# A re-searched written order up to LayerNorm 1, and the first blocks of x and context issued behind SiLU

## The chip, the cores and the metric

The kernel runs on one core of a Trainium2 chip. A core has a matrix engine (TensorE, PE in the profile), a vector engine (VectorE, DVE), a scalar engine (ScalarE, ACT), GpSimd (POOL) and SyncE (SP), each with an instruction queue of its own that runs in order. Sixteen DMA engines move data between memory and the on-chip buffer; here SP issues nearly all transfers, ScalarE a few. The metric is the device time of one execution in microseconds, the median of three runs.

## The reference

One layer of a diffusion backbone, in float32, over 256 latent tokens `x` and 256 context tokens `ctx`, width 2048. The layer computes

- `m = silu(cond) @ w_ada + b_ada`, for the sample's conditioning vector `c` and for the context's `c_ctx`, split into six vectors (shift, scale and gate for the mixer, and the same for the feed-forward part);
- `h = (x * (1 + scale) + shift) @ w_in` for latent and context tokens, the combined q/k/v projection: 3072 columns, two groups of 8 query heads with 2 key and 2 value heads each;
- attention: group A within a window with a sink logit, group B global with RMS-normalised q and k, both with axial rotary positions, keys being the latent keys and all context keys;
- `x = LayerNorm(alpha * x + gate1 * (heads @ w_out))`, LayerNorm 1;
- `x = LayerNorm(alpha * x + gate2 * ((silu(u @ w_gate) * (u @ w_up)) @ w_down))` with `u = x * (1 + scale2) + shift2`, hidden width 5632, LayerNorm 2.

## The kernel before, in words

Every large product is done as three matmuls of a float32 value split into a high and a low part: `hi*hi`, `lo*hi`, `hi*lo` (lines 240 to 242). The high part of a weight tile is a cast on ScalarE (`hi<-raw`, line 507 up to LayerNorm 1, line 230 after it), the low part a subtraction on VectorE (`lo<-raw,hi`, lines 510 and 231). The modulated tokens are split in the same way (`uh`, `ul`, lines 741 and 744).

Up to LayerNorm 1 the work is a list of about 1250 steps, each added with `F.add` for one engine. `Flow.run` goes through the string `PLAN` and emits the steps in that order; each engine keeps it (the region is a manual schedule), and steps of different engines wait for each other through semaphores only. A number is a step; a letter behind it says which pool a load takes its buffer from (`r`: four buffers, `a`: two). `wN` emits N warm-up matmuls of 128 columns into a spare bank (line 1253); each shows as two instructions in the trace.

The q/k/v projection runs over groups of the 16 blocks of 128 input columns: 2, 2, 4 and 8 blocks. For each group the shift and scale columns are computed from `w_ada` (line 558), then x and context are turned by TensorE (line 728), modulated (734), split, and multiplied with `w_in`. Ahead of the list stand the loads of the conditioning rows, a transposition of them (line 291), SiLU on ScalarE (line 294) and a tile of ones (line 306).

The steps around the start that the prediction speaks of:

| Step | Engine | What it does |
|---|---|---|
| 2, 4, 6, 8 | SP | the four first loads of w_ada, 1 MB each |
| 3, 5, 7, 9 | PE | their products with the conditioning columns, 16 matmuls each (line 558); 3 and 5 need loads 2 and 4, 7 needs 6, 9 needs 8 |
| 10 | ACT | copy of the sums (line 589), after 9 |
| 11 | PE | the sums turned into columns (line 594), after 10 |
| 0, 1 | PE, ACT | the bias b_ada transposed (line 454) and copied (line 457) |
| 12, 13 | DVE | shift and scale, from 11 and 1 (lines 600, 602) |
| 14; 19 | PE | flip of the first x block; of the first context block (line 728) |
| 15, 16, 17, 18 | ACT, ACT, ACT, DVE | x: two modulations, `uh`, `ul` |
| 20, 21, 22, 23 | ACT, ACT, ACT, DVE | the same for the context |
| 60, 67, 49, 85, 92, 78 | SP | loads of w_in for block rows 0 and 1; their casts are 61, 68, 50, 86, 93, 79 |
| 63, 70 | PE | products with the weights of 60 and of 67, the first of the old and of the new order |
| 37, 38 | ACT queue | loads of x and of the context for block group 2 (lines 699, 704) |
| 946, 1195 | POOL | two memsets |
| 1192, 1193 | SP, PE | loads of the LayerNorm rows, and their transposition |

A part of how a modulation step waits, which the table cannot say:

```python
p = F.add("PE", 205 * nj, flip, (), [ps], at=-1.0, since=9500.0)
for j in range(nj):
    p = F.add("ACT", 460, lambda j=j, f=modulate: f(j), [p] + ready, [uf] if j == 0 else [], [ps])
```

The numbers given to `F.add` were the planner's costs and due times when the order was searched for; in the kernel only the list `PLAN` decides.

After LayerNorm 1 come the gate, up and down projections in a fixed order of their own, which is the same in both kernels.

Of the kernel before, what the change touches and what calls it, by code (L numbers as in the profile page):

```python
# [21 lines left out]
P = 128  # L22
# [43 lines left out]


PLAN = """
4r 2r 1195 6a w6 3 5 0 w3 7 19 8a 946 w7 9 60r 10 1 61 14 11 1192 67r 49r 155a 27a 85r 13 12 15 16 17 20 50 68 21 22
62 18 51 w12 63 64 69 52 56 86 38 23 65 66 87 70 55 74 72 76 37 89 59 28r 78r 79 80 31r 30r 116 137r 1193 73 77 29 71  # L70
88 1194 91 156 157 32 53 33 138 99a 148r 100r 39 34 75 36 35 139 81 83 40 41 82 54 90 58 44 101 45 46 42 102r 103a 149
47 43 158 141 150 105r 92r 106a 93 162 151 104 48 57 84 145 142 143 140 144 147 94 166r 108r 109a 167 107 152 160 153
168 146 164 169 170 154 171 180r 181 182 172 110 96 115 225a 111 184 122 132 127 173r 112 95 98 226 227 228 113 114
174 175 294r 187a 188r 229 186 133 97 123 161 297 165 298 159 117 177 179 176 163 124 183 189 118 134 119 120 295 296
178 121 300 304 128 129 125 301 126 230r 231 185 315r 130 308 299 303 232 307 135 136 318 302 131 233 319 316 306 305
309 310 235a 190r 191a 311 313 312 321 234 317 236 238 237 239 192 328r 329 320 323 325 322 330 240r 314 331 242 332
334 324 338 333 337 342 349r 327 335 339 350 352 326 241 244 353 351 243 193r 245a 194r 246 247 248 250a 362r 255r 249
251 252 254 341 345 346 354 343 355 195 336 347 340 344 365 366 348 363 364 368 357 359 356 358 367 370 369 260r 196r
197r 375a 203 371 372 360 373 361 198 199 204 388 200 210 205 272 24 947 273 257 253 256 259 258 262 261 264 263 202
# [32 lines left out]
1235 1236 1161 1162 1163 1242 1164 1233 1183 1221 1222 1184 1185 1165 1189 1190 1223 1224a 1230r 1243 1225 1244 1226a  # L112
1228r 1234 1191 1227 1229 1231
"""


# [47 lines left out]
def dit_layer(ctx: ExitStack, tc: tile.TileContext, x, c, cx, c_ctx, w_ada, b_ada, w_in, q_norm_g,  # L164
              k_norm_g, sink_logit, w_out, ln1_g, ln1_b, w_gate, w_up, w_down, ln2_g, ln2_b,
              rope_cos, rope_sin, out):
    nc = tc.nc
    x, c, cx = x[0], c, cx[0]
# [11 lines left out]
    def wk_bank():  # L180
        return wk_ps.tile([P, NB], F32, tag="wk", name="wk")
# [17 lines left out]
    xt = main.tile([P, NT, D], F32, tag="xt", name="xt")  # L199
# [82 lines left out]
    brow = pa.tile([6 * KD, P], F32, tag="brow", name="brow")  # L282
    nc.scalar.dma_start(brow, b_ada.rearrange("o (n p) -> (o n) p", p=P))
    first_cx = xt[:, :, D - 2 * P :]
    nc.scalar.dma_start(xt[:, :, : 2 * P], x[:, : 2 * P].rearrange("(t p) d -> p t d", p=P))
    nc.scalar.dma_start(first_cx, cx[:, : 2 * P].rearrange("(t p) d -> p t d", p=P))
    early = wk_bank()
    for _ in range(EARLY_WARM):
        nc.tensor.matmul(early[:, :P], lhsT=ident, rhs=ident, start=True, stop=True)
# [14 lines left out]
    nc.vector.reduce_sum(fold, ident.rearrange("p (a i) -> p i a", a=4), axis=AX.X)  # L304
    ones_r = main.tile([P, P], F32R, tag="ones", name="ones")
    nc.scalar.activation(ones_r, ident, AF.Copy, bias=1.0, scale=0.0)
    ones = ones_r.bitcast(F32)


# [1556 lines left out]
```

## Time and profile before

| What | Value |
|---|---|
| median of three runs | 1119.51 us (1116.37 to 1120.67) |
| profiled execution | 1117.67 us, span 1115.9 us |
| TensorE busy | 1095.1 us, 98% of the span |
| VectorE, ScalarE busy | 895.3 us (80%), 602.6 us (54%) |
| DMA | 321.24 MB, mean 288 GB/s |
| first product of the q/k/v projection | 22.72 us after the span's start |
| last matmul | 1103.06 us after the span's start |

The span goes from the first to the last instruction; the execution's time is some microseconds longer. In the timeline a row has its start, its duration, the engine, the line, the operation, what it writes and reads, and a count; in brackets stands the idle time before it and what ended that. ACTq and SPq are the issues of transfers on the queues of ScalarE and SP. Matmuls overlap, so the time from one start to the next says more than the duration. Line numbers are those of the kernel before.

### The profile page before, as it was taken

How to read it: one execution, taken by the hardware profiler on the slowest of the kernel's cores; microseconds unless marked ns; L12 is line 12 of the kernel's file. 1: busy time of each engine (PE TensorE's matmuls, PEld its weight loads, DVE VectorE, ACT ScalarE, POOL GpSimd, SP SyncE). 2: the span in 40 equal slices, each digit the busy share in tenths (PEclk: the TensorE clock that was granted, in tenths of full speed). 3: DMA queues.
4: the chain of work that ended last, by engine and by line, in shares of the span. 5: the costliest groups of instructions: out<-in, count | busy, mean ns of one | idle time of the engine just before them, and what ended most of it. 6: DMA issues, size and time to landing. Idle time of an engine off the chain costs nothing.

```text
span 1115.9 us, 13859 instructions
## 1 busy us (share of the span) xinstructions
PE 1095.1 (98%) x5121; PEld 886.5 (79%) x5121; DVE 895.3 (80%) x1075; ACT 602.6 (54%) x874; POOL 39.4 (4%) x86
## 2 busy tenths in 40 slices
PE   7999999999999999999999999999999999999995
PEld 6677788778878788888888888888888788888884
DVE  2469999999998898877667776887875899578886
ACT  3345675786765356445465455555644565445541
POOL 1000040102000010000000000000000000000000
PEclk9999999999999999999999999999999999999998
DMA  9999998889999789989768798899896575536651
GB/s 336 383 401 392 392 338 323 298 270 315 330 323 365 275 311 357 336 295 345 265 209 280 272 342 280 295 317 312 302 308 224 174 251 206 198 141 236 233 209 75
DMA packets 175273, 321.24 MB, mean 288 GB/s; under 512 B 8899, under 2 KB 46691, under 8 KB 172901
## 3 DMA queue, kind: packets, MB, share of 16 engines
q1 hardware_dynamic: 173718, 319.23, 81.5%
q10 hardware_dynamic: 1264, 1.11, 0.3%
q8 instruction: 40, 0.66, 0.2%
q14 instruction: 27, 0.22, 0.1%
q0 software_dynamic: 224, 0.02, 0.0%
HBM read 304.07 MB, written 16.25 MB: 287 GB/s over the span
## 4 chain that ended last, share of the span: by engine, by line
PE 93%; DVE 4%; DMA 2%; ACT 1%; issue 0%; SPq 0%; DVEq 0%; ACTq 0%
PE acc L240 22%; PE acc L242 22%; PE acc L241 22%; PE wk L242 7%; PE wk L241 7%; PE wk L240 7%; PE wk L1036 2%; PE wk L558 2%; DMA raw<-in_w_ada_dram 2%; DVE adav L359 1%; PE wk L728 1%; DMA adav<-in_b_ada_dram 1%; PE acc L1253 0%; DVE lo L237 0%; DVE m L986 0%
## 5 line engine op out<-in xcount | busy, mean ns | idle before, releaser
L231 DVE TENSOR_TENSOR lo<-raw,hi 128x1024 fp32r<-128x1024 f32 x232 | 281.1, 1222 | 126.7 <-ACT hi L230 124.8
L230 ACT CAST hi<-raw 128x1024 fp32r<-128x1024 f32 x232 | 243.8, 1055 | 242.3 <-PE acc L242 130.2
L240 PE MATMUL acc<-hi,u2h 128*128 128x512 f32 x448 | 175.4, 391 | 0.0
L242 PE MATMUL acc<-hi,u2l 128*128 128x512 f32 x448 | 174.8, 390 | 0.3 <-DVE u2l L1579 0.3
L241 PE MATMUL acc<-lo,u2h 128*128 128x512 f32 x448 | 174.7, 390 | 0.0
L359 DVE SCALAR_TENSOR_TENSOR adav<-raw,cs,adav 128x1024 f32<-128x1024 f32 (+1 forms) x96 | 114.4, 1191 | 6.3 <-DMA raw<-in_w_ada_dram 2.9
L507 ACT CAST hi<-raw 128x1024 fp32r<-128x1024 f32 x84 | 87.7, 1052 | 57.8 <-PE acc L242 36.8
L510 DVE TENSOR_TENSOR lo<-raw,hi 128x1024 fp32r<-128x1024 f32 x84 | 101.3, 1222 | 10.5 <-ACT hi L507 10.3
L240 PE MATMUL acc<-hi,hTh 128*128 128x512 f32 x264 | 102.8, 390 | 0.6 <-ACT hi L236 0.6
L240 PE MATMUL acc<-hi,uh 128*128 128x512 f32 x256 | 102.9, 402 | 0.0
L241 PE MATMUL acc<-lo,hTh 128*128 128x512 f32 x264 | 102.8, 390 | 0.0
L242 PE MATMUL acc<-hi,hTl 128*128 128x512 f32 x264 | 102.7, 390 | 0.0
L242 PE MATMUL acc<-hi,ul 128*128 128x512 f32 x256 | 100.3, 392 | 0.0
L241 PE MATMUL acc<-lo,uh 128*128 128x512 f32 x256 | 99.9, 390 | 0.0
L242 PE MATMUL wk<-hi,u2l 128*128 128x512 f32 x256 | 99.8, 390 | 0.0
L241 PE MATMUL wk<-lo,u2h 128*128 128x512 f32 x256 | 99.8, 390 | 0.0
L240 PE MATMUL wk<-hi,u2h 128*128 128x512 f32 x256 | 99.7, 390 | 0.0
L242 PEld LDWEIGHTS acc<-hi,u2l 128*128 128x128 f32 x448 | 84.2, 188 | 18.1 <-DVE u2l L1579 0.7
L240 PEld LDWEIGHTS acc<-hi,u2h 128*128 128x128 f32 x448 | 84.2, 188 | 18.1 <-ACT u2h L1578 0.8
L241 PEld LDWEIGHTS acc<-lo,u2h 128*128 128x128 f32 x448 | 84.2, 188 | 17.6 <-DVE lo L231 0.4
L240 PEld LDWEIGHTS acc<-hi,uh 128*128 128x128 f32 x256 | 48.2, 188 | 15.6 <-issue 2.1
L240 PEld LDWEIGHTS acc<-hi,hTh 128*128 128x128 f32 x264 | 49.6, 188 | 11.3 <-ACT hi L236 1.0
(296 smaller groups left out, 1730.3 us busy)
## 6 DMA issues: line engine op xcount, KB each, us to landing
raw<-in_w_ada_dram SPq DMA_DIRECT2D x64, 1024.0 KB, 8.1
raw<-in_w_gate_dram SPq DMA_DIRECT2D x44, 1024.0 KB, 6.5
raw<-in_w_up_dram SPq DMA_DIRECT2D x44, 1024.0 KB, 5.5
raw<-in_w_down_dram SPq DMA_DIRECT2D x44, 1024.0 KB, 5.2
raw<-in_w_ada_dram SPq DMA_DIRECT2D x64, 512.0 KB, 5.9
raw<-in_w_in_dram SPq DMA_DIRECT2D x18, 1024.0 KB, 7.9
raw<-in_w_out_dram SPq DMA_DIRECT2D x16, 1024.0 KB, 7.1
pd<-hx SPq DMA_DIRECT2D x64, 128.0 KB, 5.3
```

The lines of the kernel that those rows point to most:

```text
L230: nc.scalar.copy(hi[:, :n], raw[:, s : s + n])
L231: nc.vector.tensor_tensor(lo[:, :n], raw[:, s : s + n], hi[:, :n].bitcast(F32), op=ALU.subtract)
L240: nc.tensor.matmul(ps, lhsT=xh, rhs=w[0], start=first, stop=False, skip_group_check=seeded)
L241: nc.tensor.matmul(ps, lhsT=xh, rhs=w[1], start=False, stop=False, skip_group_check=seeded)
L242: nc.tensor.matmul(ps, lhsT=xl, rhs=w[0], start=False, stop=last, skip_group_check=seeded)
L359: nc.vector.scalar_tensor_tensor(a[:, c : c + piece], raw[:, f : f + piece], cs[:, 4 * (g * (G4 * NB // w) + j) + 2, None], a[:, c : c + p ...
L507: nc.scalar.copy(hl.hi[:, :n], raw.t[:, s : s + n])
L510: nc.vector.tensor_tensor(hl.lo[:, :n], raw.t[:, s : s + n], hl.hi[:, :n].bitcast(F32), op=ALU.subtract)
L558: nc.tensor.matmul(bank.t[32 * j : 32 * j + 32, :width], lhsT=cs[:, 4 * k + 2 - 2 * i : 4 * k + 34 - 2 * i], rhs=raw.t[:, c * width : (c + ...
L728: nc.tensor.transpose(ps.t[:, (j * 2 + t) * P : (j * 2 + t + 1) * P], src, ident)
L1036: nc.tensor.matmul(o_ps.t[:, : 2 * P].rearrange("p (g q) -> p g q", q=32), lhsT=v, rhs=pv[:, k], start=k == 0, stop=k == 3)
```

## The change

Two edits. First, the two transfers of the first blocks of x and of the context, which ScalarE's queue issued ahead of the table load, SiLU and the ones tile, are issued behind these. Second, the string `PLAN` is replaced by another order of the same steps, with 29 units of warm-up instead of 28. No computation is added or removed. The string is cut here to its first lines.

```diff
 PLAN = """
-4r 2r 1195 6a w6 3 5 0 w3 7 19 8a 946 w7 9 60r 10 1 61 14 11 1192 67r 49r 155a 27a 85r 13 12 15 16 17 20 50 68 21 22
-62 18 51 w12 63 64 69 52 56 86 38 23 65 66 87 70 55 74 72 76 37 89 59 28r 78r 79 80 31r 30r 116 137r 1193 73 77 29 71
...
+4a 2a w11 3 6r 1195 8r 14 5 w5 7 w11 9 10 37 67r 68 946 49r 1192 85r w2 11 0 19 1 38 13 12 50 51 69 28a 27a 92r 15 16
+86 17 18 87 20 21 70 88 22 23 54 74 89 1193 72 90 76 93 52 94 58 1194 91 29 53 95 56 96 78r 30r 79 80 31r 155a 166r
...
 """
```

```diff
     brow = pa.tile([6 * KD, P], F32, tag="brow", name="brow")
     nc.scalar.dma_start(brow, b_ada.rearrange("o (n p) -> (o n) p", p=P))
     first_cx = xt[:, :, D - 2 * P :]
-    nc.scalar.dma_start(xt[:, :, : 2 * P], x[:, : 2 * P].rearrange("(t p) d -> p t d", p=P))
-    nc.scalar.dma_start(first_cx, cx[:, : 2 * P].rearrange("(t p) d -> p t d", p=P))
...
     ones_r = main.tile([P, P], F32R, tag="ones", name="ones")
     nc.scalar.activation(ones_r, ident, AF.Copy, bias=1.0, scale=0.0)
+    nc.scalar.dma_start(xt[:, :, : 2 * P], x[:, : 2 * P].rearrange("(t p) d -> p t d", p=P))
+    nc.scalar.dma_start(first_cx, cx[:, : 2 * P].rearrange("(t p) d -> p t d", p=P))
     ones = ones_r.bitcast(F32)
```

More of the change, by code (lines that the diff above doesn't have):

```diff
@@ L68 @@
 PLAN = """
-4r 2r 1195 6a w6 3 5 0 w3 7 19 8a 946 w7 9 60r 10 1 61 14 11 1192 67r 49r 155a 27a 85r 13 12 15 16 17 20 50 68 21 22
-62 18 51 w12 63 64 69 52 56 86 38 23 65 66 87 70 55 74 72 76 37 89 59 28r 78r 79 80 31r 30r 116 137r 1193 73 77 29 71
-88 1194 91 156 157 32 53 33 138 99a 148r 100r 39 34 75 36 35 139 81 83 40 41 82 54 90 58 44 101 45 46 42 102r 103a 149
-47 43 158 141 150 105r 92r 106a 93 162 151 104 48 57 84 145 142 143 140 144 147 94 166r 108r 109a 167 107 152 160 153
-168 146 164 169 170 154 171 180r 181 182 172 110 96 115 225a 111 184 122 132 127 173r 112 95 98 226 227 228 113 114
@@ L74 @@
[L74 to L78, printed above, removed]
@@ L79 @@
-197r 375a 203 371 372 360 373 361 198 199 204 388 200 210 205 272 24 947 273 257 253 256 259 258 262 261 264 263 202
[32 rows of a table removed]
-1235 1236 1161 1162 1163 1242 1164 1233 1183 1221 1222 1184 1185 1165 1189 1190 1223 1224a 1230r 1243 1225 1244 1226a
-1228r 1234 1191 1227 1229 1231
+4a 2a w11 3 6r 1195 8r 14 5 w5 7 w11 9 10 37 67r 68 946 49r 1192 85r w2 11 0 19 1 38 13 12 50 51 69 28a 27a 92r 15 16
+86 17 18 87 20 21 70 88 22 23 54 74 89 1193 72 90 76 93 52 94 58 1194 91 29 53 95 56 96 78r 30r 79 80 31r 155a 166r
@@ new lines @@
+100a 60r 97 156 157 98 57 32 81 33 82 44 39 34 35 36 61 83 84 62 71 55 59 99r 101 102r 103a 148r 63 75 45 167 40 41 46
+47 42 48 160 43 164 168 65 64 73 66 104 158 137a 105r 115 180r 138 181 139 140 144 77 141 162 182 169 170 171 172 149
+161 183 225a 108r 106a 109r 226 145 150 184 152 227 185 229 154 107 142 228 186 146 143 165 147 110 151 153 294r 295
+111 297 116 298 173a 117 112 122 315r 187r 230r 188a 174 113 114 175 296 159 132 177 179 176 127 300 123 124 118 119
+120 121 304 316 163 317 125 299 320 322 126 308 303 189 318 231 319 235a 240r 328r 232 233 236 234 178 312 190r 191a
@@ new lines @@
+321 128 129 130 133 134 135 136 131 324 307 301 237 238 311 323 329 325 305 302 326 306 309 239 330 333 331 332 337
+192 310 349r 327 334 313 352 350 341 336 345 314 338 340 342 344 335 355 348 354 245a 194r 193r 242 241 244 243 246
+247 248 353 351 195 356 339 357 343 359 358 250a 362r 255r 249 251 252 254 365 366 363 346 347 367 368 364 369 370 371
+373 361 372 260r 196r 197r 374 360 198 199 200 375a 203 204 210 205 215 257 253 256 259 258 262 261 263 264 201 202
[32 rows of a table added]
+1238 1221 1161 1236 1163 1162 1234 1222 1242 1239 1182 1183 1184 1185 1189 1164 1190 1165 1230r 1228a 1224a 1226r 1243
@@ L114 @@
+1191 1223 1244 1225 1227 1229 1231
 """
```

64 rows, old and new, of the table PLAN are left out of this document.

## The prediction

> **What bounds the kernel now.** I read the page first, then TensorE's waits, then the timeline of the first 24 us, then stretches of the span.
>
> ```profile
> PE 1095.1 (98%) x5121; PEld 886.5 (79%) x5121; DVE 895.3 (80%) x1075; ACT 602.6 (54%) x874; POOL 39.4 (4%) x86
> ```
>
> The waits of TensorE (total us, times, longest) after the first weights are there:
>
> ```profile
> PE wk L558 <- DMA raw<-in_w_ada_dram: 1.2, 1, 1.2
> PE wk L594 <- ACT ada L589: 0.7, 1, 0.7
> ...
> PE wk L1036 <- ACT pr L998: 0.3, 1, 0.3
> ```
>
> TensorE is the bound, and it hardly ever waits: 0.7 and 0.3 us between its first product and LayerNorm 1. The sum of its work is the same under the new order. So the question is when the first product of the q/k/v projection starts, and whether TensorE stalls later. TensorE's timeline up to that product (start, us, line):
>
> ```profile
> 7.76 0.28 PE L291 MATMUL wk<-ident,crow 32*128 32x32 f32 x1 [3.04 <-DMA crow<-in_c_ctx_dram]
> 7.97 2.93 PE L1253 MATMUL acc<-ident 128*128 128x128 f32 x12
> 12.07 1.93 PE L558 MATMUL wk<-raw,cs 128*32 128x256 f32 x32 [1.17 <-DMA raw<-in_w_ada_dram]
> 13.94 0.30 PE L454 MATMUL wk<-ident,brow 96*128 96x96 f32 x1
> ...
> 14.86 1.07 PE L558 MATMUL wk<-raw,cs 128*32 128x256 f32 x16
> 15.87 0.66 PE L728 MATMUL wk<-ident,xt 128*128 128x128 f32 x4
> 16.36 1.73 PE L1253 MATMUL acc<-ident 128*128 128x128 f32 x14
> 18.01 1.07 PE L558 MATMUL wk<-raw,cs 128*32 128x256 f32 x16
> 19.02 0.66 PE L728 MATMUL wk<-ident,xt 128*128 128x128 f32 x4
> 19.57 0.61 PE L594 MATMUL wk<-sel,ada 128*128 128x4 f32 x4
> 20.04 2.92 PE L1253 MATMUL acc<-ident 128*128 128x128 f32 x24
> 22.72 0.47 PE L240 MATMUL acc<-hi,uh 128*128 128x512 f32 x1
> ...
> 23.26 0.40 PE L242 MATMUL acc<-hi,ul 128*128 128x512 f32 x1
> ```
>
> L1253 are warm-up matmuls, two per unit of a "w" word; L558 with 256 columns are the four steps 3, 5 (together at 12.07), 7 and 9, that multiply the first w_ada loads; L728 are the flips of the first blocks of context and x. Before, step 9 ends at 19.02 and the first product starts at 22.72. ScalarE and VectorE in between:
>
> ```profile
> 2.46 0.58 ACTq L285 DMA_DIRECT2D xt<-in_x_dram  x1
> ...
> 3.07 1.00 ACTq L286 DMA_DIRECT2D xt<-in_ctx_dram  x1
> ...
> 8.17 0.30 ACT L306 ACTIVATE ones<-ident 128x128 fp32r<-128x128 f32 x1
> ...
> 19.15 0.37 ACT L589 COPY ada<-wk 128x256 f32<-128x256 f32 x1 [10.68 <-PE wk L558]
> ...
> 19.42 0.25 ACT L457 COPY bcol<-wk 128x96 f32<-128x96 f32 x1
> 19.55 1.06 ACT L507 CAST hi<-raw 128x1024 fp32r<-128x1024 f32 x1
> ...
> 21.68 0.62 ACT L741 CAST uh<-uf 128x512 fp32r<-128x512 f32 x1
> ...
> 22.33 0.69 DVE L744 TENSOR_TENSOR ul<-uf,uh 128x512 fp32r<-128x512 f32 x1 [0.47 <-ACT uh L741]
> 22.67 1.99 ACT L507 CAST hi<-raw 128x1024 fp32r<-128x1024 f32 x2
> ```
>
> From the copy of the modulation sums (19.15) to the finished uh (21.68 + 0.62 = 22.30) ScalarE needs 3.15 us; the first product follows its copy by 3.57, as the 24 warm-ups stand ahead of it on TensorE.
>
> **The change, part by part.**
>
> *The two transfers on ScalarE's queue.* They go behind SiLU and the ones tile (8.17), so x is issued at about 8.3 instead of 2.46 and the context at about 8.9. Leaving the front of that queue they free nothing on the path: SiLU waits for the transposition at 7.76, which waits for the row of c_ctx. When x lands comes from the issues up to 40 us (line, KB each, us from issue to landing):
>
> ```profile
> raw<-in_w_in_dram SPq DMA_DIRECT2D x8, 512.0 KB, 7.0
> xt<-in_x_dram ACTq DMA_DIRECT2D x2, 256.0 KB, 7.2
> ...
> xt<-in_ctx_dram ACTq DMA_DIRECT2D x1, 256.0 KB, 8.7
> cxt<-in_ctx_dram ACTq DMA_DIRECT2D x1, 256.0 KB, 6.2
> ...
> crow<-in_c_ctx_dram ACTq DMA_DIRECT2D x1, 8.0 KB, 6.4
> ```
>
> Whoever stood alone on the queue took 6.2 or 6.4; the first blocks took longer behind three others. I take 6.4: x lands at 14.7. The bounds are 13.3 (no wait at all, see below) and 8.3 + 8.7 = 17.0.
>
> [...]
>
> *TensorE's new order up to step 9* is w11, 3, flip of x, 5, w5, 7, w11, 9. The first 12 warm-ups take 2.93 us at 7.97 and 24 take 2.92 at 20.04, so early ones run at half the rate: w11 (22 of them) lasts until 12.6 if all of it is slow and about 12 if the rate rises on the way. I start step 3 at 12.3, its loads having landed by 12.07 even before. One group of 16 lasts 1.01 (14.86 to 15.87), a flip 0.49 (15.87 to 16.36), 14 warm-ups 1.65 (16.36 to 18.01), 0.118 each.
> - Step 3: 12.3 to 13.3. Then TensorE waits for x until 14.7; queued behind are step 5, both warm-up words, 7 and 9, and ScalarE's copy behind 9.
> - Flip of x to 15.2; step 5 to 16.2; w5 to 17.4; step 7 to 18.4; w11 to 21.0; step 9 to 22.0.
>
> That is 22.0 against 19.02: **+3.0**. Even with x there at 13.3, step 9 ends at 20.6, since 32 warm-ups and a flip now stand between the groups. That the w_ada loads may land earlier, with 0.5 MB less beside them, is worth nothing: TensorE comes to the last two at 17.4 and 21.0.
>
> *From step 9 to the first product.* ScalarE's new order is copy, issue of x block 2, cast, bias copy, issue of context block 2, cast, two modulations, cast, uh. Before, there is one cast ahead of uh, now three: two more of 1.0 each (22.67: 1.99 for two). The issues moved here cost the queue this much each:
>
> ```profile
> 27.10 0.59 ACT L793 COPY kvacc<-acc 128x512 f32<-128x512 f32 x1 [1.33 <-PE acc L242]
> 27.22 0.38 ACTq L704 DMA_DIRECT2D cxt<-in_ctx_dram  x1
> ...
> 27.58 1.05 ACT L507 CAST hi<-raw 128x1024 fp32r<-128x1024 f32 x1
> ```
>
> With an issue between, the cast starts 0.48 after the copy ahead of it; without one 0.13 to 0.27. Two issues: +0.5, part of it hidden under the copies. So 3.15 + 2.0 + 0.5 = 5.65 from copy to uh, against the 3.57 after which the first product used to start: **+2.1**. The bias transposition, now behind the sums, is ready 1.3 after the copy (sums 19.57 to 20.04, then a 0.30 transposition, as at 13.94) and the cast ahead of the bias copy ends at 1.5, so it hides; gone that cover, it would cost some tenths. The third cast's weights are issued when step 7 frees its buffer (18.4) and land 7.0 us later, 1 us ahead of their cast. I count nothing.
>
> *ul.* It is ready 0.72 after uh's end (22.33 + 0.69 less 22.30); the third matmul wants it 0.54 after the first: **+0.2**.
>
> *The rest of the order to LayerNorm 1.* There is 1.0 us of TensorE's waits to win back (0.7 and 0.3). To lose: runs of products are broken 59 times instead of 53, while all changes from one kind of TensorE work to another are 146 instead of 145. A break costs about 0.1 (14 warm-ups at the 0.112 of those from 20.04 to 22.72 end at 17.93, the group behind them starts at 18.01); I allow 0.2. Bounds −1.0 and +1.2; I take 0, as the two counts pull against each other. The block loads moved ahead have no reader before 40 us.
>
> **Sum:** 3.0 + 2.1 + 0.2 = 5.3 us. The profiled execution took 1117.67 us (span 1115.9), so it would be 1122.97; it lies 1.84 below the median of the runs, 1119.51, and on that footing the forecast is **1124.8 us**. With the bounds of x (−1.4, +2.3) and of the rest, 1122.4 to 1128.3.
>
> **The rivals.**
>
> *The clock falls back.* TensorE's last work ahead of the first product, the context's flip, ends about 2.0 after the copy; the product starts at 5.65, after 3.6 us with no warm-up in them. What idleness does stands at the span's end (last matmul; then TensorE's busy time first, granted clock third from the right):
>
> ```profile
> 1103.06 0.39 PE L242 MATMUL acc<-hilo,hTl 128*128 128x512 f32 x1
> ```
> ```profile
> 1103.00:1106.00 3.00, 0.45 (x2) 0.03 (x1) 2.38 (x5) 0.00 (x0) 0.00 (x0) 1.00 0.05 18
> 1106.00:1107.00 1.00, 0.00 (x0) 0.00 (x0) 0.89 (x7) 0.00 (x0) 0.00 (x0) 0.90 0.00 0
> ```
>
> The 0.90 in that last microsecond is half clock from 1106.8 on, 3.35 us after the last matmul. If the gap is long enough here too, the products run at half rate until the clock is granted again; at 7.97 the warm-ups ran slowly for at least 2.5 us, so some 3.4 us at half rate: +1.7, 1126.5. [...] For it: length. Against: the few tenths to spare.
>
> *x is there in time,* so that only order costs: 5.3 − 1.4 = 3.9, 1123.4. For it speaks the empty queue, against it every row above.
>
> *Not slower: the weight stream sets the pace, and TensorE catches up.*
>
> ```profile
> 6.00:11.00 5.00, 3.14 (x13) 2.81 (x13) 0.00 (x0) 0.40 (x2) 0.00 (x0) 1.00 1.09 353
> ...
> 60.00:140.00 80.00, 79.30 (x428) 57.98 (x426) 74.19 (x77) 44.59 (x71) 0.00 (x0) 1.00 1.04 394
> ```
>
> The DMA engines are full up to 140 us (share 1.04 to 1.09, 353 to 394 GB/s). If loads decide in that stretch, a late first product costs nothing there, and the weights come 0.5 MB at 375 GB/s = 1.4 us earlier: 1118.1. It decides only if TensorE waits for loads after its first product by more than the 5.3; it is busy 79.30 of 80 and its only wait for w_ada is the one at 12.07. That is the case against it.
>
> **How the numbers follow.** The forecast gets 0.55, the clock 0.15, x in time 0.18, the weight stream 0.12. Half a per cent, about what a measurement of this kernel can tell from no change, is 5.6 us: 1113.9 and 1125.1. The forecast lies just inside, so it gives 0.31 to "same" and 0.24 to "slower"; the clock 0.14 to slower and 0.01 to same; x in time 0.16 and 0.02 to same and slower; the stream 0.04 to faster, 0.08 to same. Together 0.04 faster, 0.56 same, 0.40 slower. The range reaches from part of the stream's case to the forecast's upper bound, 1119 to 1128; the likeliest case's own is 1122.4 to 1128.
>
> **What would show it.** Right: an x flip on TensorE at 14 to 15 with a DMA wait before it; step 9 ending near 22; the first L240 near 27.8, with three casts and two issues between copy and uh; no new waits to LayerNorm 1. Wrong: a first product before 25, or one as late as forecast with the span not longer, or TensorE waits of over 1 us between 30 and 390. Matmuls spaced twice as wide from the first product on are the clock's case.

## The result and the profile after

| | before | after |
|---|---|---|
| median of six runs each | 1119.09 us (1116.37 to 1120.67) | 1127.35 us (1126.52 to 1128.12) |
| profiled execution | 1117.67 us, span 1115.9 | 1128.12 us, span 1126.3 |
| first product of the q/k/v projection | 22.72 | 27.18 |
| first product of the gate and up projections | 383.38 | 391.83 |
| last matmul | 1103.06 | 1113.03 |

The ratio is 1.0077, with a 95% interval of 1.0063 to 1.0091: slower by 8.3 us where 5.3 were forecast, and 2.5 us above the forecast time. The two profiled spans lie 10.4 us apart; the table parts them: +4.46 to the first product, +3.99 from there to LayerNorm 1's first reader, +1.52 from there to the last matmul, and +0.4 behind it. That is one pair of traces: the start of the kernel after stands unchanged in `e4b_new_start` and `e6_old_tail` below, and their first products come at 26.46 and 26.16.

TensorE's timeline of the kernel after, up to its first products (line numbers between 285 and 306 are two lower than before):

```profile
12.09 1.07 PE L558 MATMUL wk<-raw,cs 128*32 128x256 f32 x16
14.15 0.66 PE L728 MATMUL wk<-ident,xt 128*128 128x128 f32 x4 [1.00 <-DMA xt<-in_x_dram]
14.74 1.07 PE L558 MATMUL wk<-raw,cs 128*32 128x256 f32 x16
...
17.05 1.07 PE L558 MATMUL wk<-raw,cs 128*32 128x256 f32 x16
18.05 2.72 PE L1253 MATMUL acc<-ident 128*128 128x128 f32 x22
20.70 1.07 PE L558 MATMUL wk<-raw,cs 128*32 128x256 f32 x16
...
27.18 0.79 PE L240 MATMUL acc<-hi,uh 128*128 128x512 f32 x1 [3.73 <-ACT uh L741]
27.77 0.63 PE L241 MATMUL acc<-lo,uh 128*128 128x512 f32 x1
28.20 0.63 PE L242 MATMUL acc<-hi,ul 128*128 128x512 f32 x1
...
31.91 0.40 PE L242 MATMUL acc<-hi,ul 128*128 128x512 f32 x1
```

Step 9, the last of the four w_ada products, starts at 20.70 and ends about 21.70 (as the next instruction's start has it); x is waited for until 14.15. From 27.77 on the products start 0.43 apart and last 0.63, then from 31.91 on 0.40: the first ten ran at half clock, the eleventh in part. The stretches of the span say the same (TensorE's busy time first after the length, then its weight loads, VectorE, ScalarE, GpSimd, the granted clock, the DMA share, GB/s); the limits are those at which the clock's records change, and multiples of 3.413 us from them; between the changes, at 11.28, 24.93, 31.76 and 1117.20, lie 4, 2 and 318 times that:

```profile
11.28:14.69 3.41, 2.41 (x28) 1.52 (x26) 0.00 (x0) 0.00 (x0) 0.00 (x0) 1.00 1.10 348
...
18.11:21.52 3.41, 3.41 (x40) 2.89 (x38) 0.00 (x0) 0.00 (x0) 0.00 (x0) 1.00 0.77 213
21.52:24.93 3.41, 1.93 (x21) 1.47 (x13) 0.37 (x3) 2.78 (x5) 0.00 (x0) 1.00 1.01 350
24.93:28.35 3.42, 1.17 (x3) 0.94 (x4) 3.41 (x4) 3.39 (x7) 0.00 (x0) 0.50 1.06 365
28.35:31.76 3.41, 3.41 (x10) 2.64 (x9) 1.24 (x2) 0.94 (x2) 0.00 (x0) 0.50 1.05 382
```

The clock is halved from 24.93 to 31.76. Twelve products take 4.73 us from 27.18 to 31.91, where the kernel before takes 2.59 for its first twelve (22.72 to 25.31): **2.1 us** are lost there. ScalarE between the copy of the sums and the first `uh`:

```profile
21.84 0.37 ACT L589 COPY ada<-wk 128x256 f32<-128x256 f32 x1 [13.55 <-PE wk L558]
21.85 0.46 ACTq L699 DMA_DIRECT2D xt<-in_x_dram  x1
22.35 1.05 ACT L507 CAST hi<-raw 128x1024 fp32r<-128x1024 f32 x1
23.06 0.61 ACTq L704 DMA_DIRECT2D cxt<-in_ctx_dram  x1
...
23.71 1.04 ACT L507 CAST hi<-raw 128x1024 fp32r<-128x1024 f32 x1 [0.18 <-issue]
24.66 1.02 ACT L734 ACTIVATE uf<-wk,shc,scc 128x256 f32<-128x256 f32 x2
25.57 1.04 ACT L507 CAST hi<-raw 128x1024 fp32r<-128x1024 f32 x1
26.51 0.62 ACT L741 CAST uh<-uf 128x512 fp32r<-128x512 f32 x1
```

Three casts and two issues stand between copy and `uh`, and `uh` is done at 27.13. TensorE's waits of the kernel after (total us, times, longest):

```profile
PE acc L240 <- ACT uh L741: 3.7, 1, 3.7
...
PE wk L728 <- DMA xt<-in_x_dram: 1.6, 2, 1.0
PE wk L1403 <- DVE xt L1184: 1.4, 1, 1.4
...
PE acc L240 <- ACT u2h L1578: 0.6, 1, 0.6
PE wk L728 <- DMA cxt<-in_ctx_dram: 0.3, 1, 0.3
```

Against the trace of before, these are new behind the start: 0.60 and 0.29 for the third group's blocks of x and of the context, and at LayerNorm 1 0.56 for `u2h` and 1.38 for the normalised x. The first two come and go between executions: the kernel before, traced again (`before_again`), has 0.20 and 0.29 at the same place. Their places in the timeline:

```profile
137.43 1.06 PE L594 MATMUL wk<-sel,ada 128*128 128x4 f32 x8 [0.70 <-ACT ada L589]
139.09 1.06 PE L728 MATMUL wk<-ident,xt 128*128 128x128 f32 x8 [0.60 <-DMA xt<-in_x_dram]
140.44 1.07 PE L728 MATMUL wk<-ident,cxt 128*128 128x128 f32 x8 [0.29 <-DMA cxt<-in_ctx_dram]
...
391.83 0.50 PE L240 MATMUL acc<-hi,u2h 128*128 128x512 f32 x1 [0.56 <-ACT u2h L1578]
...
397.61 0.63 PE L1403 MATMUL wk<-ident,xt 128*128 128x128 f32 x4 [1.38 <-DVE xt L1184]
```

Before, the same three rows around the flips stand closer:

```profile
130.69 1.06 PE L594 MATMUL wk<-sel,ada 128*128 128x4 f32 x8 [0.70 <-ACT ada L589]
131.60 1.07 PE L728 MATMUL wk<-ident,xt 128*128 128x128 f32 x8
132.51 1.04 PE L728 MATMUL wk<-ident,cxt 128*128 128x128 f32 x8
```

From the sums' columns to the second flip it is 1.82 us before and 3.01 after: **1.2 us**, of which the printed idle times make 0.9. So the span's +10.4 is 4.46 (start) + 2.1 (clock) + 1.2 (third group's flips) + 0.6 (`u2h`) + 1.5 (the wait for the normalised x, 1.4 of it) + 0.4 behind the last matmul, which leaves 0.1.

The theory I took to the chip: the new order's first 301 steps cost most of the loss, through the later first product and the half clock; the order behind them costs the rest; the moved transfers cost nothing. The rivals: that the moved transfers are to blame, that the weight stream takes back whatever the start wins or loses, and that the order behind the start is harmless.

### The profile page after: what moved, and what is told of

Its sections match the earlier page's. It is cut to its first block, busy times and chain, and to the rows that moved or that the text cites. A ratio compares the mean times of both kernels' runs of the same rounds, so it can differ in the third digit from the quotient of the medians.

```text
span 1126.3 us, 13871 instructions
## 1 busy us (share of the span) xinstructions
PE 1099.1 (98%) x5123; PEld 887.4 (79%) x5123; DVE 894.9 (79%) x1075; ACT 603.0 (54%) x874; POOL 46.8 (4%) x86
## 4 chain that ended last, share of the span: by engine, by line
PE 75%; issue 18%; DVE 4%; POOL 2%; DMA 0%; ACT 0%; DVEq 0%; POOLq 0%; ACTq 0%
PE acc L241 17%; PE acc L240 17%; PE acc L242 17%; PE wk L242 7%; PE wk L241 7%; PE wk L240 6%; PE wk L1036 2%; POOL cosQ L430 1%; DVE lo L510 1%; DMA raw<-in_w_ada_dram 0%; DVE lo L237 0%; PE wk L377 0%; POOL sinQ L435 0%; PE wk L1435 0%; DVE raw L1727 0%
```

## The experiments

Medians are set against the kernel before run beside them on the same chip; differences between two experiments carry an uncertainty of one to two microseconds. The kernel before took 1119.09 us beside the kernel after and 1118.14 to 1119.04 beside the experiments. Both orders hold the same set of steps in their first 301 places, and again in their first 1138, so they can be cut and joined there.

### The transfers alone (`e1_dma_only`)

```diff
     first_cx = xt[:, :, D - 2 * P :]
-    nc.scalar.dma_start(xt[:, :, : 2 * P], x[:, : 2 * P].rearrange("(t p) d -> p t d", p=P))
-    nc.scalar.dma_start(first_cx, cx[:, : 2 * P].rearrange("(t p) d -> p t d", p=P))
...
     nc.scalar.activation(ones_r, ident, AF.Copy, bias=1.0, scale=0.0)
+    nc.scalar.dma_start(xt[:, :, : 2 * P], x[:, : 2 * P].rearrange("(t p) d -> p t d", p=P))
+    nc.scalar.dma_start(first_cx, cx[:, : 2 * P].rearrange("(t p) d -> p t d", p=P))
```

The order stays that of before.

> The written order of the kernel before, with the two transfers moved behind SiLU. Theory 'start' (the loss is the new order's longer way to the first product, plus the clock that falls back in the gap before it): the move alone costs nothing, since x is flipped at 19.0 and the context at 15.9 in this order; first product at 22.2 to 23.0, 1118.5 to 1120 us. Rival 'transfers' (x and context coming late is what costs): TensorE waits at the context's flip for 1 us or more, first product after 23.7, 1121 us or more.

Measured: 1117.08 us (1116.58 to 1117.78, 10 runs), before 1119.04 (1117.01 to 1123.32, 22 runs), ratio 0.9979 (0.9969 to 0.9990). The moved transfers lose nothing; with the old order they win about 2 us, more than was expected. Yet the two profiled spans are alike, 1115.6 and 1115.9. What differs is the scatter, to which the traces under `before_again` return.

### The order alone (`e2_order_only`)

```diff
     first_cx = xt[:, :, D - 2 * P :]
     nc.scalar.dma_start(xt[:, :, : 2 * P], x[:, : 2 * P].rearrange("(t p) d -> p t d", p=P))
     nc.scalar.dma_start(first_cx, cx[:, : 2 * P].rearrange("(t p) d -> p t d", p=P))
...
-PLAN = the order of before
+PLAN = the order of after
```

> The new written order, with the two transfers ahead of SiLU as before. Theory 'start': the wait of 1.0 us for x at its flip goes, the rest stays: first product near 26.2, clock still falls back in the gap, about 1126.3 us. Rival 'transfers': the loss goes, 1119 to 1121 us.

Measured: 1126.26 us (1124.71 to 1127.73), ratio 1.0058 (1.0038 to 1.0079). The order carries nearly all of the loss. With x early the wait ahead of its flip is gone, but the first product stands at 25.80, and the clock is halved from 25.97 to 29.38. The two edits do not add up: the order alone costs 7.2 us and the transfers alone win 2.0, but together they cost 8.3. Under the new order the moved transfers win nothing; the first product comes at 25.80 with x early and at 26.16 to 27.18 with x late.

### Warm-ups in the gap (`e3_warm_gap`)

```diff
-... w2 11 0 19 1 38 13 12 50 51 ...
+... w2 11 0 19 w16 1 38 13 12 50 51 ...
```

> The changed kernel with 16 units of warm-up matmuls (32 instructions, 3.6 us at the full clock) behind the context's flip, in the gap ahead of the first product. Theory 'clock' (the gap lets the clock fall and the products from 27.2 to 31.6 run at half rate): products 0.227 us apart from the first on, first product still near 27.2, 2.2 us less than the changed kernel, about 1125.2 us. Rival (the slow products only use slack that a later wait would have taken): same time as the changed kernel, 1127.3 us.

Measured: 1125.92 us (1124.05 to 1127.42), ratio 1.0056 (1.0036 to 1.0076), 1.4 below after. TensorE's timeline of this kernel:

```profile
22.57 3.74 PE L1253 MATMUL acc<-ident 128*128 128x128 f32 x32
26.23 0.50 PE L240 MATMUL acc<-hi,uh 128*128 128x512 f32 x1
26.57 0.40 PE L241 MATMUL acc<-lo,uh 128*128 128x512 f32 x1
...
139.48 0.63 PE L241 MATMUL acc<-lo,uh 128*128 128x512 f32 x1
```

The first products run at full rate, the second in 0.40 us where after has 0.63: with 3.74 us of warm-ups in the gap the clock is not halved there. But the trace shows 0.63 again at 139.48. The stretch ahead of it is that of the third group's flips with their waits:

```profile
133.97:137.38 3.41, 2.16 (x17) 1.89 (x18) 3.41 (x6) 3.38 (x5) 0.00 (x0) 1.00 1.05 404
137.38:140.79 3.41, 3.41 (x13) 3.02 (x14) 3.41 (x4) 2.46 (x7) 0.00 (x0) 0.50 1.05 387
```

Here a second weak place of the new order, with TensorE busy for 2.16 us of a window, halved the clock too. In the trace of after the same place did not; its two windows there held 2.72 and 2.52 us. The half clock at the start is worth 2.1 us by the rows of after. The 1.4 us of the medians are no clean price for it: in this trace the first product also comes 0.95 us earlier than in that of after, where none was expected, and the half clock comes back at 137.38.

### The old start, the new rest (`e4_old_start`)

```diff
-PLAN = the order of after
+PLAN = the first 301 steps of the order of before, then the rest in the order of after
```

> The first 301 steps in the order of the kernel before, the rest in the new order, transfers moved as in the change. Theory 'start': first product near 22.5, no fall of the clock; what is left is the waits at LayerNorm 1 (some 2 us more than before), 1120.5 to 1122 us. Rival 'rest' (the order behind the start carries the loss): 1124 us or more.

Measured: 1120.66 us (1119.7 to 1121.48), ratio 1.0012 (1.0001 to 1.0023). Giving back the old start alone wins 6.7 of the 8.3 us. Against `e1_dma_only`, which has both starts and rest of before, the new rest costs 3.6. Its waits:

```profile
PE wk L1403 <- DVE xt L1184: 1.4, 1, 1.4
...
PE acc L240 <- ACT u2h L1578: 0.6, 1, 0.6
```

The two waits at LayerNorm 1 stay, so they belong to the rest of the order and not to its late start. They are 2.0 of the 3.1 us by which this profiled span (1118.7) is longer than that of `e1_dma_only` (1115.6); 0.3 more lie behind the last matmul, and for the remaining 0.8 the trace has no single wait. The waits for the third group's x and context are gone, as they are from `e4b_new_start`, `e6_old_tail` and `e8_few_warm`; the last two have the new order at that place, so the order alone does not bring them.

### The new start, the old rest (`e4b_new_start`)

```diff
-PLAN = the order of after
+PLAN = the first 301 steps of the order of after, then the rest in the order of before
```

> The kernel after with its first 301 steps in the new order and all later steps to LayerNorm 1 in the order of before; transfers of x and context moved. The counterpart of the old start (1120.66). If start and rest add up: the rest of the new order cost 1120.66 - 1117.08 = 3.6, so here 1127.35 - 3.6 = 1123.8; no waits of TensorE for the third group's x near 139, none for the normalised x near 397, first product near 27 with the clock fallen. If the rest's loss comes only from being late behind the old start's loads, the new start keeps some of it: 1125 or more. If the loss of the start is given back where the loads decide: below 1121.

Measured: 1124.76 us (1123.56 to 1127.97), before 1118.14, ratio 1.0067 (1.0046 to 1.0089). By the medians the rest is worth 2.6 here and 3.6 in its counterpart; measured from the kernel before beside each run it is 1.6 here (8.3 less 6.6). The time lies between the two that were expected, 1123.8 and 1125, so whether start and rest simply add up stays open. No wait for the normalised x or for `u2h` of line 240 is left; the first product stands at 26.46 at half clock. The rival that the weight stream gives the start back is ruled out: 1121 was its bound.

### Casts behind `uh` (`e5_casts_behind`)

```diff
-... 13 12 50 51 69 28a 27a 92r 15 16 86 17 18 87 20 21 70 88 22 23 54 74 ...
+... 13 12 69 28a 27a 92r 15 16 17 18 70 71 86 87 50 51 20 21 88 22 23 54 75 74 ...
```

> The changed kernel with the casts of steps 50 and 86 (and their VectorE halves) moved behind uh, the product of step 71, which needs neither, pulled up to second place, and its evacuation with it. Theory 'casts' (two casts more ahead of uh make the first product 2 us late): first product 2.0 us earlier than in the changed kernel, near 25.2, gap ahead of it 1.8 instead of 3.7 us, so that the clock holds; 3 to 4 us less than the changed kernel, 1123.3 to 1124.3 us. Rival 'all casts are needed anyway' (the next products wait for what was moved): first product near 25.2, but waits of about 2 us in the next products, 1125 to 1127 us.

Measured: 1127.41 us (1127.1 to 1127.47), ratio 1.0074 (1.0056 to 1.0091): no gain. TensorE's timeline, the stretch that holds the gap, and a wait that the kernel after does not have:

```profile
22.66 0.60 PE L728 MATMUL wk<-ident,xt 128*128 128x128 f32 x4
25.36 0.50 PE L240 MATMUL acc<-hi,uh 128*128 128x512 f32 x1 [2.10 <-ACT uh L741]
...
27.16 0.63 PE L240 MATMUL acc<-hi,uh 128*128 128x512 f32 x1
```

```profile
23.66:27.07 3.41, 1.71 (x6) 1.14 (x7) 2.54 (x3) 3.38 (x5) 0.00 (x0) 1.00 1.08 385
27.07:30.48 3.41, 3.41 (x9) 2.66 (x9) 2.80 (x4) 2.16 (x5) 0.00 (x0) 0.50 1.07 404
```

```profile
PE wk L558 <- DMA raw<-in_w_ada_dram: 1.1, 1, 1.1
```

The first product comes 1.82 us earlier than in the trace of after, of the 2.0 that moving two casts behind `uh` was to give; from the copy of the sums to it are 3.71 us instead of 5.34. Then the clock falls for one window, after a gap of only 2.10, and at 52.30 TensorE waits 1.1 us for w_ada. Both prices were missing from what I expected, and the time lies above both ranges; the earlier start is not kept. Why the load is late is open: `e3_warm_gap` runs the same products at 50.39 without a wait.

### The new order with the tail of before (`e6_old_tail`)

```diff
-PLAN = the order of after
+PLAN = the first 1138 steps of the order of after, then the order of before
```

> The changed kernel to step 1138 of the order, the rest in the order of before. Theory 'LayerNorm 1' (the new order's end makes TensorE wait 1.4 us for the normalised x and 0.6 us for u2h): both waits go, 1.5 to 2.0 us less than the changed kernel, about 1125.5 us. Rival: the steps ahead of 1138 are late already and the waits stay, 1127 us.

Measured: 1125.02 us (1124.27 to 1125.09), ratio 1.0052 (1.0037 to 1.0067): 2.3 below after. Neither wait at LayerNorm 1 is in its trace. The order of the last hundred steps makes them, 0.6 + 1.4 by the rows.

### Fewer warm-ups in the old start (`e7_dma_trim`)

```diff
-... 7 ... w7 ... 62 18 51 w12 63 ...
+... 7 ... w3 ... 62 18 51 w9 63 ...
```

On the kernel with the transfers moved and the order of before; the word `w7` stands ahead of step 9.

> The order of before with the two transfers moved, warm-up word w7 cut to w3 and w12 to w9. If step 9 and the first product stand behind warm-ups longer than behind their data, step 9 starts near 17.1 instead of 17.9 and the first product near 21.6 instead of 22.6: 1116 us, 1 us less than with the transfers alone (1117.1). Rival: the fourth load of w_ada lands at 17.8 to 18 in many executions and nothing is gained, 1117 us.

Measured: 1116.99 us (1116.24 to 1118.53), against 1117.08 of `e1_dma_only`. The first product is 1.8 us earlier (20.88), and the waits hold a new line:

```profile
PE wk L558 <- DMA raw<-in_w_ada_dram: 1.2, 1, 1.2
```

The second of the line 558 groups behind the start begins at 38.78 instead of 38.95, and this is where the wait stands. The rival's time holds, but not its place: step 9 starts at 16.53 without a wait. So in this trace the weight stream takes back nearly all of a start earlier than that of the kernel before.

### Fewer warm-ups in the new start (`e8_few_warm`)

```diff
-... 14 5 w5 7 w11 9 10 ...
+... 14 5 7 w3 9 10 ...
```

> The changed kernel without w5 and with w3 in place of the second w11. Theory 'warm-ups in the way' (step 9 ends 2 to 3 us later than its load allows because of the flip of x and the 32 warm-ups): step 9 ends near 18.6 instead of 21.7, first product near 24.0; the gap ahead of it is as long, so the clock still falls; about 1124.2 us. Rival 'load-bound': the first product waits for the w_in load of step 85 or the fourth w_ada load instead, first product after 25.5, 1126 us or more.

Measured: 1125.17 us (1124.82 to 1125.33), ratio 1.0054 (1.0039 to 1.0069): 2.2 below after. The first product stands at 23.53, 3.65 earlier, still at half clock for one window. The trace has two waits that after does not have. One, 0.65 us for w_ada at 17.11, stands ahead of step 9 and so is already in the time of the first product. The other, 1.2 us behind LayerNorm 1 (line 675), cannot be put down to the earlier start: `before_again`, whose start is late, has 1.5 us there. The 3.65 are counted from the latest of the three traces of the new start; from the other two it is 2.6 and 2.9, and 2.2 are won at the end.

### Both mends (`e9_few_warm_old_tail`)

```diff
-... 14 5 w5 7 w11 9 10 ...          steps behind place 1138 in the order of after
+... 14 5 7 w3 9 10 ...              steps behind place 1138 in the order of before
```

> The kernel after with word w5 left out and the second w11 made w3 (together -2.2 us in its own run) and with the steps behind number 1138 in the order of before (-2.3 us in its own run). If the two places are independent: 1127.35 - 2.2 - 2.3 = 1122.9, first product near 23.5, no wait of line 1403 for the normalised x. If what the shorter start wins is taken by a later wait: 1125.

Measured: 1122.94 us (1122.66 to 1123.79), ratio 1.0045 (1.0030 to 1.0060). The sum expected was 1122.9: the two mends add up, within what these runs can tell. Even mended, the new order stays 4.8 us behind the old one; a gap of 4.41 us ahead of the first product and a half clock from 23.24 to 26.65 are left.

### The kernel before, traced again (`before_again`, `before_again2`)

> The kernel before, unchanged, for a second trace. Its runs scatter from 1116.4 to 1120.7 us while those with only the transfers moved lie within 1116.6 to 1117.8. If the scatter comes from the start (where the transfers stand in front), a slower execution shows a later first product or a TensorE wait for w_ada or x ahead of it; if from anything later, the first product stands near 22.7 and the milestones part behind it.

> As the run ahead of it, a third trace of the kernel before: the same reading.

Measured: 1121.03 and 1119.28 us, with the first product at 24.41 and 24.24 instead of 22.72. In the second that is nearly all of the longer span (1.5 of 1.6 us). In the first it is half (1.7 of 3.4); 1.5 more lie in a wait at 418.81, far from the start, that neither of the other two traces of this kernel has:

```profile
PE wk L675 <- DVE part L1100: 1.5, 1, 1.5
```

So part of the scatter comes from the start and part does not. TensorE's timeline of the first of them:

```profile
11.49 3.64 PE L558 MATMUL wk<-raw,cs 128*32 128x256 f32 x32 [0.83 <-DMA raw<-in_w_ada_dram]
...
16.55 1.07 PE L558 MATMUL wk<-raw,cs 128*32 128x256 f32 x16
```

The 32 matmuls of steps 3 and 5 take 3.64 us, where the first trace had 1.93: they run wholly at half clock. The clock is granted at 16.29 here and at 15.61 in the other trace; it was 11.11 in the first. The stretch that ends one window ahead of the grant, and the one at whose end the first trace had it:

```profile
9.46:12.88 3.42, 2.59 (x22) 1.71 (x25) 0.00 (x0) 0.00 (x0) 0.00 (x0) 1.00 1.09 379
```

```profile
7.70:11.11 3.41, 3.14 (x13) 2.81 (x13) 0.00 (x0) 0.40 (x2) 0.00 (x0) 1.00 1.08 354
```

(The 1.00 of these rows is no reading: the clock's records begin with the first change.) A window with 3.14 us of TensorE's work was followed by the full clock, one with 2.59, in which TensorE had waited for w_ada, was not. With the transfers moved that wait is not there, in `e1_dma_only`:

```profile
10.67 3.25 PE L558 MATMUL wk<-raw,cs 128*32 128x256 f32 x32
...
22.64 0.48 PE L240 MATMUL acc<-hi,uh 128*128 128x512 f32 x1
```

Steps 3 and 5 follow the warm-ups at once, 0.8 us earlier than in `before_again`, no window after the first is broken, and the clock was granted at 13.40. `e4_old_start` and `e7_dma_trim`, with the same transfers and first steps, do not have the wait either; their clock was granted at 12.71 and 12.42. So what the moved transfers win at the start is read like this: the w_ada loads are there when the warm-ups end, and the clock came at the end of the window from 9.99 to 13.40, in which TensorE worked for all of its 3.41 us; in `before_again` the wait broke the window from 9.46 to 12.88 (2.59 us of work), and the clock came one window later, at 16.29. These are three traces against three, and no run took the wait away by other means. The size fits the two later traces of before (1.6 and 1.8 us of first product against 2.0 of median) and not the first, which had the early grant and the wait all the same; so the cause of the two microseconds is argued, not shown.

## Why the prediction was right and wrong, point by point

Slower was right, the forecast of 1124.8 was 2.5 us too low, and "the clock falls back", to which I gave 0.15, is what happened, together with losses that the forecast put at nothing. By the prediction's own line of half a per cent the result is "slower", which had 0.40, and not "same", which had 0.56. That the time lies inside 1119 to 1128 is in part luck: the upper bound allowed for a later x and a small loss in the rest, but x came as forecast, and the clock and a larger loss in the rest filled that room.

- *x lands at 14.7.* Right: it was issued at 7.90 and its flip could start at 14.15, about 6.2 us after the issue. The rival "x in time" is ruled out.
- *Step 9 ends at 22.0, +3.0.* Right: about 21.70, +2.7. Each row of the working lies 0.2 to 0.6 earlier than written. One term was mis-sized without effect: by the prediction's own rows 22 slow warm-ups from 7.97 last until about 12.9 (22 times twice 0.112), not 12.6; in `e5_casts_behind`, where all of them ran slow, they took 4.99 us.
- *From copy to first product, 5.65, +2.1.* Right: 5.34 (21.84 to 27.18), +1.8. The issues hid under the copies more than allowed.
- *ul, +0.2.* Not seen: at half clock the third product starts 1.02 after the first, and `ul` is ready by then.
- *The first product at 27.8.* 27.18 in this trace, 26.46 and 26.16 in the two others with the same start. The start was mis-sized by 0.6 to 1.6, on the high side.
- *The clock.* Here the step failed. I set the length of the gap, 3.6 us, against the 3.35 that lie between the last matmul and the half clock in the trace of before. It was 3.73 long, from 23.45 to 27.18, but the clock fell 1.48 into it, at 24.93, after a window of 3.41 us with 1.93 us of work in it. `e5_casts_behind` with its gap of 2.10 shows that the wrong thing was asked: there the clock fell after a window with 1.71 us of work. How little work in a window is enough, these traces do not settle (last section), so the chance of a fall could not have been computed from them. All seven kernels with the new start and no warm-ups in the gap lost the clock there, so 0.15 was too low. The price had been put at +1.7; it is 2.1. The 3.4 us at half rate behind the +1.7 were my estimate, which the 2.5 us of slow warm-ups beside it do not show; the clock of the kernel after was at half for 6.83 us, 4.58 of them with products (27.18 to 31.76).
- *The rest of the order to LayerNorm 1, taken as 0, bounds −1.0 and +1.2.* Here the sum failed. It lost 1.6 to 3.6 us by the two cut and joined orders. Counting breaks between kinds of work could not see it: 2.0 us are two waits at LayerNorm 1, for `u2h` (0.6) and for the normalised x (1.4), which every trace with the new order's tail has and none with the old one; `e6_old_tail` wins them back. The 0.9 for the third group's blocks in the trace of after is no part of it that can be counted on, and what makes up the remainder is open. In the trace of after the waits at LayerNorm 1 come behind 390 us, where the sign to watch for ended.
- *The weight stream sets the pace.* Mostly wrong. A late start was not caught up (`e4b_new_start`, 1124.76 us), so its 1118.1 fell. But a start 1.8 us earlier than that of before was given back at a load of w_ada (`e7_dma_trim`, 1.2 us of wait). In the window from 18.11 to 21.52 the DMA engines moved 213 GB/s instead of the 371 of the window ahead of it: by the rows, no load is issued between 11.80 and 18.18, when step 7 has ended. What this costs later no run shows.
- *The footing.* The profiled execution of before, 1117.67, had the early grant of the clock. Two later traces, without it, took 1119.28 and 1121.03. So against a typical execution part of the +4.46 at the start was already paid. With the profiled execution of after, 1128.12, the slowest of its six, this is how the profiled spans can lie 10.4 apart and the medians 8.3.
- *Transfers that leave ScalarE's front free nothing.* Wrong in the good direction: with the old order they gain 2 us; TensorE then does not wait for w_ada ahead of its first product, and the clock is granted by 13.40. I had priced the earlier landing at nothing because under the new order TensorE comes late; under the new order they indeed gain nothing (`e2_order_only` is 1.1 us faster than after).

Behind the last matmul every kernel with the new middle (places 302 to 1138) needs 13.2 to 13.4 us to the end, every kernel with the old one 12.8 to 12.9. The engines' last rows stand at the same distance in both (the four output transfers are issued 7.33 us after the last matmul's start); why they finish 0.4 later is open.

The best kernel of these is the one with the transfers moved and the order of before, 0.9979 of before (0.9969 to 0.9990); with fewer warm-ups besides (`e7_dma_trim`) it is as fast.

## What to carry to other kernels

When an order is replaced, price the waits that it opens at every hand-over, not only the start: follow each first reader of a group back through the queues of the engines that feed it. Where TensorE has a hole, ask what work is left in the clock's windows around it, and not only how long the hole is: here some windows with 1.43 to 2.16 us of work in 3.41 were followed by half clock. And before a start is shortened or filled, find what holds the next milestone: here leaving out 26 warm-ups ahead of needed products won 2.2 us under the new order, while under the old one a start 1.8 us earlier was given back at a load. Before a single trace is explained, trace the same kernel again: two of three traces of before differed from the first by 1.5 to 1.7 us at the start alone.

## What the runs showed of the hardware

Between one change of the granted clock and the next lay whole multiples of 3.413 us, here called windows: 321 in the trace of before, between its first and its last change (11.11 and 1106.79), and 4, 2 and 318 in that of after. Some windows, with their limits counted from the clock's changes in each trace:

| Window | Kernel | TensorE busy, us of 3.41 | Clock after it |
|---|---|---|---|
| 7.70 to 11.11 | before | 3.14 | goes to full |
| 23.24 to 26.65 | both mends | 2.95 | goes to full |
| 25.41 to 28.83 | new order, tail of before | 2.67 | stays at half |
| 9.46 to 12.88 | before, traced again | 2.59 | stays at half |
| 11.28 to 14.69 | after | 2.41 | stays full |
| 133.97 to 137.38 | warm-ups in the gap | 2.16 | falls to half |
| 388.18 to 391.60 | old start, new rest | 2.01 | stays full |
| 21.52 to 24.93 | after | 1.93 | falls to half |
| 415.65 to 419.06 | before, traced again | 1.90 | stays full |
| 23.66 to 27.07 | casts behind `uh` | 1.71 | falls to half |
| 1108.97 to 1112.38 | fewer warm-ups, new start | 1.57 | stays full |
| 1101.27 to 1104.68 | fewer warm-ups, old start | 1.43 | falls to half |

In the fourteen traces the grant came behind windows with 2.95 us of work or more, and behind none with 2.67 or less. For the fall there is no such line: windows with 1.43 to 2.16 us of work were followed by half clock, but other windows with 1.57 to 2.01 us kept the full clock. One of these, and the window behind it, with the clock third from the right:

```profile
415.65:419.06 3.41, 1.90 (x17) 1.27 (x15) 3.31 (x5) 2.96 (x4) 1.87 (x3) 1.00 0.83 252
419.06:422.48 3.42, 3.42 (x18) 2.85 (x19) 3.38 (x4) 1.03 (x2) 2.31 (x4) 1.00 1.05 399
```

So TensorE's busy time alone does not decide. Nor does the kind of work sort them plainly: the window with 2.16 us holds flips and 4-column products, but one from 9.58 to 13.00 of both mends, with 2.07 us of warm-ups, w_ada products and flips, kept the clock. What decides is open. I had not expected that a wait for w_ada in the first twelve microseconds would go with a grant 4.5 or 5.2 us later in two of three traces of the same kernel, and a first product 1.5 to 1.7 us later: the first trace of before waited 1.17 us, 0.96 of them behind the window with 3.14 us of work, and had the early grant; the other two waited 0.83 and 1.03, inside windows with 2.59 and 2.39 us, and had the late one.
